# A projection on TensorE: the v channels of the first stage with tokens stationary, and gates as extra columns

## The chip, the cores and the metric

The kernel runs on one core of one Trainium2 chip. The metric is the device time of the whole program in microseconds (us). The core has a matrix engine (TensorE, PE in the profile; PEld is its loading of stationary operands), a vector engine (VectorE, DVE), a scalar engine (ScalarE, ACT) and GpSimd (POOL). SyncE (SP) only issues transfers here. Matmuls write their sums to PSUM, which is used as 8 banks of 128 partitions x 512 fp32 values; all other tiles are in SBUF.

## The reference

One layer of an encoder over two sequences, 1024 and 256 tokens of width 2048. The parts that bear on the change:

```python
hn = rmsnorm(x, norm_w)
proj = einsum('btd,dp->btp', hn, w_in)            # 2048 -> 4*1024 + 5*1024 + 16 columns
na_q, na_k, na_v, na_g, ml_qk, ml_v, ml_o, ml_z, ml_gp = split(proj, ...)
att = neighbourhood_attention(na_q, na_k, na_v, na_rpb) * silu(na_g)
q, k = split(silu(centred_depthwise_conv(ml_qk, conv_w, conv_b)), 2)
gates = ml_gp.reshape(B, T, 2, 2, ML_HEADS) + gate_b           # the 16 columns
mem = rmsnorm(bidirectional_mlstm(q, k, ml_v, gates)) * sigmoid(ml_o) * silu(ml_z)
y = rmsnorm(x + einsum('btm,md->btd', concat(att, mem), w_out), final_norm_w)
```

All data are fp32. na_v and ml_v are 1024 channels each, 2048 v channels together.

## The kernel before

**Precision.** Each fp32 operand of a projection is split into a high part of a reduced format (F32R) and the rest. A product is three matmuls into the same sums: high by high, high by low, low by high. Splitting weights costs a cast on ScalarE (L184) and a subtraction on VectorE (L185, both in `split_a`).

**Stages.** The 1280 tokens are two groups: A with 768 and B with 512. The first stage (up to 1096 us) projects group A to all channels; the second (1096 to 2149 us) projects group B, with the attention and the mLSTM among it; then follows the output projection (L1654).

**A pair.** The first stage goes through the channels in pairs of 128-channel blocks. `pair_a(n1)` computes blocks n1 and n1+1 for all 768 tokens, with the names `A<n1>...` in the profile. It uses a Strassen-like scheme over a 2x2x2 cut (two halves of K, two halves of the tokens, two blocks): seven products, in the order 1, 5, 6, 4, 7, 2, 3, instead of eight. Weights are stationary (128x128) and 384 tokens move. A product has 8 K steps of 3 matmuls, so a pair has 168 matmuls, and its result has channels on partitions. For the products 5, 6, 7 and 3 the weight operand is a sum of raw weights, formed by GpSimd (L531). The sums of tokens are formed once and stay in SBUF; `xop(i, kk, part)` gives the one of product i.

Buffers: raw weights "ra" (3 of 512 KB, one per quarter of K), sums "wt" (4), split weights "wsa" (8), results "pc" (5). A pair holds seven banks, three of tag "pr" and four of the five of tag "a". At the end of K its banks are folded into four result quarters: L498 copies product 1, L494 adds the others, and L263 (`scaled`) multiplies by the tokens' norm.

**What follows a pair.** `finish_a` is a generator, run in steps among the next pair's work. For mLSTM q/k pairs (numbers 24, 26, ... 38) it is the convolution: per block one ScalarE activation, four taps on VectorE (L424), tanh (L429), L430, and a split and store (L180, L181, `store_conv`). For v pairs (56, 58, ... 70) it transposes on TensorE (L470): per 128 tokens two 128x128 transposes into a bank, then `store_v` splits and stores rows of tokens to DRAM.

**Gates.** `gates_a`, called behind the second pair (A6), computes the 16 gate columns of the 768 tokens with 64 wide and 12 small matmuls (L591, L599) and adds the bias (L600). It takes one "ra", four "wsa" and one "pc" buffer.

**Order.** Pairs are issued as 4, 6, and then for i = 0 to 7: q/k pair 24+2i, v pair 56+2i, two others. So A56 comes behind A24, A60 behind A28, and so on. Within this order a planner of the framework interleaves each engine's instructions, by a simulated timeline; dependencies become semaphore waits. The first stage's v in the second stage's form is already in the program for group B: `proj_v` (L769) keeps 128 tokens stationary and moves 256 weight columns, 272 for the unit that has the gates with it. Its results need no transpose.

Of the kernel before, what the change touches and what calls it, by code (L numbers as in the profile page):

```python
# [47 lines left out]
def kernel(  # L48
# [23 lines left out]
    def f(ap):  # L72
        return ap.bitcast(F32)

    def bank(tag, name):
        return ps.tile([P, 512], F32, tag=tag, name=name, bufs=3 if tag == "pr" else 5)
# [103 lines left out]
            S.mul(hi, src, scale)  # L180
            return V.scalar_tensor_tensor(lo, src, scale, f(hi), op0=ALU.mult, op1=ALU.subtract)  # L181

    def split_a(hi, lo, src):
        S.copy(hi, src)  # L184
        last_split["ins"] = V.tensor_tensor(lo, src, f(hi), op=ALU.subtract).ins  # L185

    def q_view(ap):
        return ap.rearrange("p (b r c) -> p r b c", b=4, c=16)
# [44 lines left out]
    def store_v(u, t0, o, src, scale=None):  # L233
        if u >= NA_H // 2:
            hi, lo = o[:, 0], o[:, 1]
        else:
            hi, lo = (o.rearrange("p a (j d) -> p (a j) d", j=2).rearrange(
                "p (j z) d -> p z j d", z=2)[:, z] for z in range(2))
            src = src.rearrange("p (j d) -> p j d", j=2)
        split(hi, lo, src, scale)  # L240
        flat = f(o).rearrange("p a d -> p (a d)")
        if u >= NA_H // 2 or t0 >= TP:
            DM.dma_start(vS[u][t0 : t0 + P], flat)
            return
# [44 lines left out]
        return wa.tile([P, GA], F32, tag="pc", name=name, bufs=NPC)  # L289

    def wsa(name):
        return wa.tile([P, 2, 256], F32R, tag="wsa", name=name, bufs=NWS)

    def first_tiles():
        names = ("pr", "pr", "pr", "a", "a", "a", "a", "a")
# [41 lines left out]
        for kk in range(8):  # L337
            wr = wa.tile([P, 1024], F32, tag="ra", name=f"fr{kk}", bufs=NRA)
            wv = wr.rearrange("p (g j f c) -> p g j f c", g=2, j=2, f=2)
            load(kk, 0)  # L340
            for g_ in range(2):
                DM.dma_start(
                    wv[:, g_],
                    w_in[g_, kk // 2].rearrange("p (j f q c) -> p j f q c", j=2, f=2, q=2)[
                        :, :, :, kk % 2, :
                    ],
                )
            load(kk, 1)
            ws = {}

            def wsplit(h):
                for g_ in range(2):
                    t = wsa(f"fw{kk}_{h}{g_}")
                    hi, lo = (t[:, z].rearrange("p (j c) -> p j c", j=2) for z in range(2))
# [79 lines left out]
    def finish_a(n1, Cn):  # L434
        nm = f"A{n1}"
        for j in range(2):
            if n1 >= NCH:
                break
# [24 lines left out]
        if n1 >= NCH:  # L463
            yield
            yield
            yield
            for tt in range(GA // P):
                b = bank("a", f"{nm}v{tt}")
                for j in range(2):
                    PE.transpose(b[:, j * P : (j + 1) * P], Cn[j][:, tt * P : (tt + 1) * P], ident)  # L470
                if tt in (1, 3):
                    vo = wa.tile([P, GA], F32R, tag="pc", name=f"{nm}vo{tt}", bufs=NPC)
                    vo = vo[:, :512].rearrange("p (a d) -> p a d", a=2)
                else:
                    vo = wa.tile([P, 2, 256], F32R, tag="vo", name=f"{nm}vo{tt}", bufs=1)
                store_v((n1 - NCH) // 2, tt * P, vo, b[:, :256])
                yield

    def pair_a(n1, bg=iter(()), hook=None, first=False, pinned=False):
        nm = f"A{n1}"  # L480
# [37 lines left out]
        for r in range(4):  # L518
# [16 lines left out]
            for i in order:  # L535
# [13 lines left out]
                split_a(t[:, 0], t[:, 1], src[i])  # L549
                for q in range(2):  # L550
                    kk = 2 * r + q
                    mm_c(
# [11 lines left out]
            pass  # L564
        return finish_a(n1, Cn)

    def gates_a():
        raw = wa.tile([P, 1024], F32, tag="ra", name="gAw", bufs=NRA)
        DM.dma_start(raw[:, :256], w_g)
        ab = [raw[:, :P], raw[:, P : 2 * P]]  # L570
        ext = [raw[:, 256 : 256 + P], raw[:, 384 : 384 + P]]
        V.tensor_tensor(ext[0], ab[0], ab[1], op=ALU.add)
        V.tensor_scalar(ext[1], ab[0], -1.0, None, op0=ALU.mult)
        st = []
        for i, src in enumerate((*ab, *ext)):
            t = wsa(f"gAt{i}").rearrange("p h c -> p (h c)")[:, : 8 * 32 + 96]
            G.memset(f(t), 0.0)
            tv = t[:, :256].rearrange("p (k h c) -> p k h c", h=2, c=16)
            sv = src.rearrange("p (k c) -> p k c", c=16)
            split_a(tv[:, :, 0, :], tv[:, :, 1, :], sv)  # L580
            st.append(t)
        sel = raw[0:32, 512:528]
        V.tensor_tensor(sel, ident[0:32, 0:16], ident[0:32, 16:32], op=ALU.add)
        gs = pc("gAg")
        for th, prods in enumerate((((0, 1), (1, 2)), ((2, 3), (3, 7)))):
            b = bank("a", f"gAb{th}")[:, :HALF]
            n = 0
            for w_, i in prods:
                for kk in range(8):
                    for hl_ in range(2):  # L590
                        PE.matmul(  # L591
                            b, st[w_][:, kk * 32 : kk * 32 + P], xop(i, kk, hl_),
                            start=n == 0, stop=n == 31,
                        )
                        n += 1
            V.tensor_copy(gs[0:32, th * HALF : (th + 1) * HALF], b[0:32])
        for tt in range(GA // P):
            b = bank("a", f"gAt{tt}")
            PE.matmul(b[:, :16], gs[0:32, tt * P : (tt + 1) * P], sel, start=True, stop=True)  # L599
            V.scalar_tensor_tensor(  # L600
                gt[:, tt, :], b[:, :16], rcs[0][:, tt : tt + 1], gb_sb, op0=ALU.mult, op1=ALU.add
            )

    opening = first_tiles()
    next(opening)
# [19 lines left out]

    bg = opening
    for i, n1 in enumerate(order):
        bg = pair_a(n1, bg, second_pools if i == len(order) - 1 else None, i == 0, i == 1)
# [109 lines left out]
    def proj_v(u, X):  # L738
# [7 lines left out]
            outs = [pb[t // 2][:, (t % 2) * 256 : (t % 2) * 256 + 256] for t in range(nt)]  # L746
        for r in range(4):
            raw = w_piece(w_in[NCH // 2 + u, r], f"v{u}_{r}")
            rawv = raw.rearrange("p (j f q c) -> p f q j c", j=2, f=2, q=2)
# [5 lines left out]
            for f_ in range(2):  # L755
                t = wb.tile([P, 2, 544], F32R, tag="wsp", name=f"wsv_{u}_{r}_{f_}", bufs=4)
                t4 = t[:, :, : 2 * w].rearrange("p h (k c) -> p h k c", k=2)
                h2, l2 = (
                    t4[:, z, :, 0:256].rearrange("p q (j c) -> p q j c", j=2) for z in range(2)
                )  # L760
                split(h2, l2, rawv[:, f_])
# [979 lines left out]
def _layout(inputs):  # L1741
# [8 lines left out]
    for name, n in (("q", 1024), ("k", 1024), ("v", 1024), ("g", 1024), ("qk", 2048),  # L1750
# [5 lines left out]
    w_in = np.ascontiguousarray(  # L1756
        ch.reshape(2, 4, 2, P, nb // 2, 2, P).transpose(4, 1, 3, 5, 0, 2, 6).reshape(nb // 2, 4, P, 1024)
    )
    gorder = [d * 8 + w_ * 4 + h for w_ in range(2) for d in range(2) for h in range(4)]
    w_g = np.ascontiguousarray(  # L1760
        cols["gp"][:, gorder].reshape(KT, P, 16).transpose(1, 0, 2).reshape(P, KT * 16)
# [65 lines left out]
```

## Time and profile before

| what | value |
|---|---|
| median of 3 runs | 2550.02 us (2548.44 to 2554.36) |
| profiled execution | 2548.95 us |
| span in its profile | 2547.2 us |
| TensorE busy, matmuls | 2527.0 us (99%), 15126 |
| VectorE busy | 1978.3 us (78%) |
| ScalarE busy | 1349.3 us (53%) |
| GpSimd busy | 591.4 us (23%) |
| first stage, second stage, output projection | to 1096, to 2149, to the end |

A row of the chain of waits gives start, length, engine, tile and line, and after the x the number of instructions. A row of the timeline has the same with the operation, what it writes and reads, and the shape; in brackets stands the idle time ahead of it and what ended it. A row of a tile gives the shortest, median and longest duration in ns. Since matmuls overlap in the array, one matmul's recorded duration is longer than the time between two starts.

### The profile page before, as it was taken

The page shows a single profiled execution, that of the slowest core. Times are in us where ns is not written, and L with a number is a line of the kernel's source. Part 1 is how long each engine was busy: PE and PEld are TensorE (multiplying, and loading weights), DVE is VectorE, ACT ScalarE, POOL GpSimd, SP SyncE. Part 2 cuts the span into 40 slices and gives each one's busy share as a digit, 9 for nine tenths or more (in the row PEclk, how much of TensorE's full clock was granted, in tenths as well). Part 3 has the DMA queues.
Part 4 walks back from the last instruction along what each step waited for, and adds up shares of the span by engine and source line. Part 5 has one row for each costly group of instructions (what it writes and reads, how often), then busy time and mean ns, then how long its engine had stood idle before and what let it go on. Part 6 is the DMA issues. An engine that isn't in the chain of part 4 may idle for free.

```text
span 2547.2 us, 44753 instructions
## 1 busy us (share of the span) xinstructions
PE 2527.0 (99%) x15126; PEld 2366.8 (93%) x15126; DVE 1978.3 (78%) x4040; ACT 1349.3 (53%) x3051; POOL 591.4 (23%) x894
## 2 busy tenths in 40 slices
PE   8999999999999999999999999999999999999998
PEld 8999999999999999999999899899898888888886
DVE  8768888898969798988875676776875665889695
ACT  8635545444444444475655665666665653344445
POOL 0434545444444444510000011010100103000001
PEclk9999999999999999999999999999999999999999
DMA  6556474636433343476778888888877849646227
GB/s 216 159 160 206 137 233 132 182 120 192 130 115 128 108 129 100 133 246 210 232 248 270 268 267 288 276 260 272 299 223 242 286 129 356 199 149 211 88 87 256
DMA packets 307757, 505.67 MB, mean 199 GB/s; under 512 B 48992, under 2 KB 195080, under 8 KB 307528
## 3 DMA queue, kind: packets, MB, share of 16 engines
q1 hardware_dynamic: 304568, 491.01, 60.2%
q0 software_dynamic: 2960, 11.80, 1.2%
q8 instruction: 120, 1.97, 0.3%
q14 instruction: 109, 0.89, 0.1%
HBM read 374.18 MB, written 128.52 MB: 197 GB/s over the span
## 4 chain that ended last, share of the span: by engine, by line
PE 83%; DMA 2%; DVE 1%; ACT 1%; issue 0%; SPq 0%; ACTq 0%; POOLq 0%; POOL 0%
PE po L1654 15%; PE pc L686 15%; PE pv L769 5%; PE A16b L286 1%; PE A52b L286 1%; PE A44b L286 1%; PE A40b L286 1%; PE A20b L286 1%; PE A48b L286 1%; PE A50b L286 1%; PE A42b L286 1%; PE A18b L286 1%; PE A14b L286 1%; PE A54b L286 1%; PE A70b L286 1%; PE A68b L286 1%
## 5 line engine op out<-in xcount | busy, mean ns | idle before, releaser
L1654 PE MATMUL po<-wo,mo 128*128 128x512 f32 x1620 | 375.6, 393 | 0.0
L1654 PEld LDWEIGHTS po<-wo,mo 128*128 128x128 f32 x1620 | 304.1, 188 | 70.5
L178 DVE TENSOR_TENSOR ws<-wr,ws 128x512 fp32r<-128x512 f32 x144 | 98.5, 693 | 40.0 <-ACT ws L177 39.5
L177 ACT CAST ws<-wr 128x512 fp32r<-128x512 f32 x144 | 87.6, 617 | 67.7 <-PE pc L686 55.5
L177 ACT CAST mo<-mb 128x640 fp32r<-128x640 f32 x72 | 52.0, 726 | 110.6 <-PE po L1654 100.1
L118 POOL TENSOR_SCALAR rs<-rs 128x1 f32<-128x1 f32 x10 | 4.4, 440 | 373.6 <-DVE rs L1628 373.4
L178 DVE TENSOR_TENSOR mo<-mb,mo 128x640 fp32r<-128x640 f32 x72 | 59.0, 825 | 31.3 <-ACT mo L177 31.3
L1597 DVE TENSOR_TENSOR y<-y,po 128x512 f32<-128x512 f32 x90 | 58.0, 684 | 13.2 <-PE po L1654 13.0
L177 ACT CAST mo<-ms 128x640 fp32r<-128x640 f32 x40 | 28.9, 725 | 50.7 <-PE po L1654 32.6
L178 DVE TENSOR_TENSOR wsv<-wr_v,wsv 128x512 fp32r<-128x512 f32 x64 | 44.6, 702 | 14.1 <-ACT wsv L177 13.9
L177 ACT CAST wsv<-wr_v 128x512 fp32r<-128x512 f32 x64 | 38.9, 617 | 24.5 <-PE pv L769 13.0
L424 DVE SCALAR_TENSOR_TENSOR pcv<-pco,cw_sb,pcv 128x516 f32<-128x516 f32 x48 | 36.5, 760 | 8.5 <-ACT pcv L418 8.5
L1611 ACT ACTIVATE jk<-y 128x512 f32<-128x512 f32 x40 | 25.2, 630 | 29.8 <-DVE y L1597 29.5
L178 DVE TENSOR_TENSOR mo<-ms,mo 128x640 fp32r<-128x640 f32 x40 | 32.9, 823 | 9.8 <-ACT mo L177 9.8
L131 ACT ACTIVATE xq<-xq 128x1024 f32<-128x1024 f32 x20 | 21.2, 1060 | 34.3 <-DMA xq<-in_xtok_dram 32.0
L1110 POOL MEMSET mls_0v<- 128x2 f32 x4 | 0.4, 102 | 162.5 <-DVE S_dt.float L178 137.1
L286 PE MATMUL fb<-xg,fw 128*128 128x384 f32 x192 | 34.6, 334 | 0.0
L286 PEld LDWEIGHTS fb<-xg,fw 128*128 128x128 f32 x192 | 33.4, 188 | 0.0
L807 DVE CUSTOM_DVE_ANT_0 nap_0st<-nap_0s,nap_0bt 128x384 f32<-128x384 f32 x32 | 17.7, 553 | 19.8 <-PE nap_0s L802 7.8
L1560 DVE TENSOR_TENSOR ms<-mb,mb 128x640 f32<-128x640 f32 x40 | 32.9, 823 | 0.0
L263 DVE TENSOR_TENSOR pco<-pc,rstdb 128x512 f32<-128x512 f32 x28 | 19.1, 687 | 16.7 <-PE pc L686 15.8
L810 ACT ACTIVATE nap_0st<-nap_0st,nap_0sm 128x384 f32<-128x384 f32 x32 | 19.8, 617 | 21.9 <-DVE nap_0sm L807 21.9
(2770 smaller groups left out, 8507.5 us busy)
## 6 DMA issues: line engine op xcount, KB each, us to landing
wr<-in_w_in_dram SPq DMA_DIRECT2D x72, 512.0 KB, 4.9
wr_v<-in_w_in_dram SPq DMA_DIRECT2D x32, 512.0 KB, 5.0
wb<-in_w_o_dram SPq DMA_DIRECT2D x48, 256.0 KB, 3.4
xq<-in_xtok_dram SPq DMA_DIRECT2D x20, 512.0 KB, 4.1
mb<-mx POOLq DMA_DIRECT2D x32, 320.0 KB, 7.9
y<-in_xtok_dram SPq DMA_DIRECT2D x35, 256.0 KB, 5.3
wr_wp<-in_w_o_dram SPq DMA_DIRECT2D x16, 512.0 KB, 6.5
vS<-vo SPq DMA_DIRECT2D x24, 256.0 KB, 5.2
```

The lines of the kernel that those rows point to most:

```text
L131: S.activation(raw, raw, AF.Square, accum_out=ssq[g][:, t, q : q + 1])
L177: S.copy(hi, src)
L178: return V.tensor_tensor(lo, src, f(hi), op=ALU.subtract)
L286: PE.matmul(o, w(a_), x(b_), start=first and m == 0, stop=last and m == 2)
L424: V.scalar_tensor_tensor(dst[:, a:n], src[:, a + j - pad : n + j - pad], cw_sb[:, ct, j : j + 1], dst[:, a:n], op0=ALU.mult, op1=ALU.add,)
L686: PE.matmul(pb[j], t[j][:, wi, c : c + P], xs[xi], start=first and m == 0, stop=last and m == 2,)
L769: PE.matmul(outs[tt], xs[:, tt * P : (tt + 1) * P], t[:, wi, q * w : (q + 1) * w], start=first and m == 0 and (gates or tt % 2 == 0), stop ...
L810: S.activation(st, st, AF.Exp, bias=sm[:, 0:1], scale=-1.0, accum_out=sm[:, 2:3])
L1560: V.tensor_tensor(t, x, y_, op=op)
L1597: V.tensor_tensor(Y[p, q, tt], Y[p, q, tt], bk, op=op)
L1611: S.activation(jk, Y[p, q, tt], AF.Square, accum_out=ss[t][:, c : c + 1])
L1654: PE.matmul(bk[tt], m[xi][:, tt * P : (tt + 1) * P], w[wi], start=first and kk == 0 and j == 0, stop=last and j == 2, skip_group_check=True,)
```

## The change

The eight v pairs of the first stage become four units of 512 channels, `unit_v(u, ...)` with u = 0, 2, 4, 6 and names `V<u>...`. A unit takes the place of the pair that had stood there for even i; those of odd i are left out. The same seven products are made with the roles exchanged: 128 tokens (of a half of 384: three tiles) are stationary and 256 weight columns move, so the result has tokens on partitions. A product has 3 tiles x 8 K steps x 3 = 72 matmuls, a unit 504. A tile's 256 columns fill half a bank, and `place` lays a product's third tile beside another product's.

- The products of a unit are made in two passes over K, (1, 5, 6, 7, 3) and then (2, 4), since the banks don't hold all seven. The weights are loaded as 512 KB per K step in two transfers of 1-KB runs (`whole`), and the second half of K again for the last pass.
- V0 also carries the 16 gate columns. They are in the products 1, 2, 3 and 7, whose tiles are then 272 wide and take a bank each. V0 therefore has three passes, (1, 7, 5), (6, 3) and (2, 4), and loads and sums weights anew in the second (`V0p`). For each such product and K step the 16 columns are split apart from the weights (one more ScalarE and one more VectorE instruction). `gate` adds them up with the bias on VectorE.
- `gates_a`, the transposes, and the scaling of v by L263 go. `finish_v` scales by the tokens' norm in the store's split. The gate weights have a buffer of their own.
- The v weights lie in another order in DRAM, and `proj_v` of the second stage reads them without a rearrangement.

```diff
-    order += [QK0 + 2 * i, NCH + 2 * i, *rest[2 * i : 2 * i + 2]]
+    order += [QK0 + 2 * i, *((NCH + 2 * i,) if i % 2 == 0 else ()), *rest[2 * i : 2 * i + 2]]
...
+        if n1 >= NCH:
+            bg = unit_v((n1 - NCH) // 2, bg, gw if n1 == NCH else None)
+        else:
+            bg = pair_a(...)
         if i == 1:
-            gates_a()
+            gw = gate_weights()
...
+    def finish_v(u, z, C):
+        for tt in range(3):
+            t = 3 * z + tt
...
+            store_v(u, t * P, vo, C[:, tt * 256 : (tt + 1) * 256], rcs[0][:, t : t + 1])
+            yield
...
+        def product(i, kk, src, b):
+            t = wsa(f"{nm}s{kk}{i}")
+            split_a(t[:, 0, :256], t[:, 1, :256], src)
+            w = 256
+            if i in G_OF:
+                w = 272
+                split_a(t[:, 0, 256:], t[:, 1, 256:], gw[:, G_OF[i], kk], -1.0 if i == 7 else None)
+            for tt, (o, own, closes) in enumerate(b[i][0]):
+                for m, (xi, wi) in enumerate(((0, 0), (0, 1), (1, 0))):
+                    PE.matmul(
+                        o, xop(i, kk, xi)[:, tt * P : (tt + 1) * P], t[:, wi, :w],
+                        start=kk == 0 and own and m == 0, stop=kk == 7 and closes and m == 2,
+                    )
...
+        for kk in range(8):
+            A, src = whole(kk, "r"), {}
+            for i in passes[0][0]:
+                src[i] = source(i, kk, A, src)
+                product(i, kk, src[i], b)
+                if kk < 7:
+                    if i in (5, 7):
+                        next(bg, None)
+                    continue
+                if i == 1:
+                    for _ in bg:
+                        pass
+                    new(0)
+                    gate(1, b)
+                    for c, o in b[1][1][1:] if gw is None else b[1][1]:
+                        S.copy(C[0][:, c], o)
...
+        if gw is not None:
+            V.tensor_tensor(gw[:, 0], gw[:, 0], gw[:, 1], op=ALU.add)
+            b = {6: place(6, "pr", bank("a", f"{nm}h1")), 3: place(3, ("pr", "pr", "a"))}
+            for kk in range(8):
+                A, src = whole(kk, "p"), {}
+                for i in (5, 6, 3):
+                    src[i] = source(i, kk, A, src)
+                    if i in b:
+                        product(i, kk, src[i], b)
...
+            b = {2: place(2, ("a",) * 3), 4: place(4, "pr", bank("a", f"{nm}h3"))}
```

How the instructions stand is shown at three places; a row is line, operation, written<-read tiles and shape. First, TensorE between A6 and A24. Before, the end of the gate block (`gAb`, `gAt`) stands ahead of A24:

```order
L591 MATMUL gAb_1768<-xg_6_269,gAt_1728 128x384 x2
L591 MATMUL gAb_1768<-xg_7_273,gAt_1728 128x384 x2
L599 MATMUL gAt_1802<-gAw,gAg 128x16
L599 MATMUL gAt_1805<-gAw,gAg 128x16
L599 MATMUL gAt_1808<-gAw,gAg 128x16
L286 MATMUL A24b_1820<-xb_242,A24s_1829 128x384 x3
L286 MATMUL A24b_1820<-xb_246,A24s_1829 128x384 x3
```

Now, on the same engine and at the same place:

```order
L285 MATMUL A6b_1364<-xg_7_271,A6s_1688 128x384 x3
L285 MATMUL A6b_1365<-xg_6_267,A6s_1701 128x384 x3
L285 MATMUL A6b_1365<-xg_7_271,A6s_1701 128x384 x3
L285 MATMUL A24b_1714<-xb_242,A24s_1723 128x384 x3
L285 MATMUL A24b_1714<-xb_246,A24s_1723 128x384 x3
```

A24 follows A6 directly. Second, TensorE at the turn from V0's first pass to its second, now (`V0b` and `V0h` are banks, `V0s` split weights, `xb` and `xg` stationary tokens; bank 2497 is product 6 of the second pass, 2498 to 2500 product 3):

```order
L498 MATMUL V0b_2_2068<-V0s_2454,xg_7_273 128x272 x3
L498 MATMUL V0b_2070<-V0s_2477,xg_7_272 128x256 x6
L498 MATMUL V0h_2069<-V0s_2477,xg_7_272 128x256 x3
L498 MATMUL V0b_2497<-V0s_2508,xg_0_244 128x256 x6
L498 MATMUL V0b_2497<-V0s_2543,xg_1_248 128x256 x6
L498 MATMUL V0b_2497<-V0s_2578,xg_2_252 128x256 x6
L498 MATMUL V0b_0_2498<-V0s_2522,xg_0_243 128x272 x3
L498 MATMUL V0b_1_2499<-V0s_2522,xg_0_243 128x272 x3
```

Before, the same engine at the end of A56, in whose place V0 stands, goes on to the pair A8:

```order
L286 MATMUL A56b_2174<-xg_7_271,A56s_2479 128x384 x3
L286 MATMUL A56b_2175<-xg_6_267,A56s_2492 128x384 x3
L286 MATMUL A56b_2175<-xg_7_271,A56s_2492 128x384 x3
L286 MATMUL A8b_2510<-xb_242,A8s_2519 128x384 x3
L286 MATMUL A8b_2510<-xb_246,A8s_2519 128x384 x3
L286 MATMUL A8b_2511<-xg_0_244,A8s_2531 128x384 x3
L286 MATMUL A8b_2511<-xg_1_248,A8s_2531 128x384 x3
```

What moved: behind the first 216 matmuls, not behind the whole of the v work, TensorE now begins new sums in a bank that was just written. Third, VectorE at that turn, now (`A24cv` is the convolution of A24, `gt` the gates, `V0c` the results of V0):

```order
L423 SCALAR_TENSOR_TENSOR A24cv_2227<-A24c_1973,cw_sb,A24cv_2227 128x766
L178 TENSOR_TENSOR V0s_2522<-gw,V0s_2522 128x16
L178 TENSOR_TENSOR V0s_2543<-V0t_2541,V0s_2543 128x256
L178 TENSOR_TENSOR V0s_2557<-V0t_2555,V0s_2557 128x256
L178 TENSOR_TENSOR V0s_2557<-gw,V0s_2557 128x16
L536 SCALAR_TENSOR_TENSOR gt<-V0b_0_2063,rstdc_229,gb_sb 128x16
L429 SCALAR_TENSOR_TENSOR A24cv_2227<-A24c_1973,A24cv_2227 128x766
L178 TENSOR_TENSOR V0s_2578<-V0t_2576,V0s_2578 128x256
L536 SCALAR_TENSOR_TENSOR gt<-V0b_1_2064,rstdc_229,gb_sb 128x16
```

Before, on the same engine, beside A56:

```order
L424 SCALAR_TENSOR_TENSOR A24cv_2326<-A24c_2079,cw_sb,A24cv_2326 128x766
L185 TENSOR_TENSOR A56s_2492<-A56t_2490,A56s_2492 128x256
L185 TENSOR_TENSOR A8s_2519<-A8r_2517,A8s_2519 128x256
L430 SCALAR_TENSOR_TENSOR A24cv_2326<-A24c_2079,A24cv_2326 128x766
L185 TENSOR_TENSOR A8s_2531<-A8t_2528,A8s_2531 128x256
L185 TENSOR_TENSOR A8s_2543<-A8t_2540,A8s_2543 128x256
L494 TENSOR_TENSOR A56c_2416<-A56c_2416,A56b_2171 128x384
```

The read of V0's first bank (`gt<-V0b_0_2063`) stands behind the taps of A24's convolution. On ScalarE, now, the copies of V0's product 1 to its result stand behind the convolution's last activation:

```order
L428 ACTIVATE A24c_1973<-A24cv_2227 128x766
L177 CAST V0s_2578<-V0t_2576 128x256
L177 CAST V0s_2592<-V0t_2590 128x256
L177 CAST V0s_2592<-gw 128x16
L180 ACTIVATE A24ch_2329<-A24cv_2227 128x766
L573 COPY V0c_2445<-V0b_0_2063 128x256
L573 COPY V0c_2445<-V0b_1_2064 128x256
```

More of the change, by code (lines that the diff above doesn't have):

```diff
@@ L181, in split, with split_a @@
             return V.scalar_tensor_tensor(lo, src, scale, f(hi), op0=ALU.mult, op1=ALU.subtract)
-    def split_a(hi, lo, src):
-        S.copy(hi, src)
-        last_split["ins"] = V.tensor_tensor(lo, src, f(hi), op=ALU.subtract).ins
+    def split_a(hi, lo, src, scale=None):
+        last_split["ins"] = split(hi, lo, src, scale).ins
     def q_view(ap):
@@ L291, in wsa @@
     def wsa(name):
-        return wa.tile([P, 2, 256], F32R, tag="wsa", name=name, bufs=NWS)
+        return wa.tile([P, 2, 272], F32R, tag="wsa", name=name, bufs=NWS)
     def first_tiles():
@@ L353, in wsplit @@
                     t = wsa(f"fw{kk}_{h}{g_}")
-                    hi, lo = (t[:, z].rearrange("p (j c) -> p j c", j=2) for z in range(2))
+                    hi, lo = (t[:, z, :256].rearrange("p (j c) -> p j c", j=2) for z in range(2))
                     split_a(hi, lo, wv[:, g_, :, h, :])
@@ L462, in finish_a @@
             yield
-        if n1 >= NCH:
-            yield
[L465 to L477, printed above, removed]
+    def finish_v(u, z, C):
+        for tt in range(3):
+            t = 3 * z + tt
+            if True:
+                vo = wa.tile([P, GA], F32R, tag="pc", name=f"V{u}o{t}", bufs=NPC)
+                vo = vo[:, :512].rearrange("p (a d) -> p a d", a=2)
+            else:
+                vo = wa.tile([P, 2, 256], F32R, tag="vo", name=f"V{u}o{t}", bufs=1)
+            store_v(u, t * P, vo, C[:, tt * 256 : (tt + 1) * 256], rcs[0][:, t : t + 1])
+            yield
@@ L565, in pair_a, with gate_weights @@
         return finish_a(n1, Cn)
[L567 to L602, printed above, removed]
+    def gate_weights():
+        gw = wa.tile([P, 2, 8, 16], F32, tag="gw", name="gw", bufs=1)
+        DM.dma_start(gw, w_g.rearrange("p (f k c) -> p f k c", f=2, c=16))
+        return gw
     opening = first_tiles()
@@ L748, in proj_v @@
             raw = w_piece(w_in[NCH // 2 + u, r], f"v{u}_{r}")
-            rawv = raw.rearrange("p (j f q c) -> p f q j c", j=2, f=2, q=2)
+            rawv = raw.rearrange("p (f q c) -> p f q c", f=2, q=2)
             if gates:
@@ L757, in proj_v @@
                 t4 = t[:, :, : 2 * w].rearrange("p h (k c) -> p h k c", k=2)
[L758 to L761, printed above, removed]
+                split(t4[:, 0, :, 0:256], t4[:, 1, :, 0:256], rawv[:, f_])
                 if gates:
@@ L1758, in _layout @@
     )
+    vw = w_in[NCH // 2 :].reshape(NU, 4, P, 2, 2, 2, P).transpose(0, 1, 2, 4, 5, 3, 6)
+    w_in[NCH // 2 :] = vw.reshape(NU, 4, P, 1024)
     gorder = [d * 8 + w_ * 4 + h for w_ in range(2) for d in range(2) for h in range(4)]
```

125 lines of the change are left out of this document (121 added, 4 removed).

## The prediction

> **What bounds the kernel now.** I read the page first: the busy shares, the granted clock and the make-up of the chain that ended last.
>
> ```profile
> span 2547.2 us, 44753 instructions
> PE 2527.0 (99%) x15126; PEld 2366.8 (93%) x15126; DVE 1978.3 (78%) x4040; ACT 1349.3 (53%) x3051; POOL 591.4 (23%) x894
> PEclk9999999999999999999999999999999999999999
> PE 83%; DMA 2%; DVE 1%; ACT 1%; issue 0%; SPq 0%; ACTq 0%; POOLq 0%; POOL 0%
> ```
>
> TensorE is the bound, at an undisturbed clock. That is an average, so next comes the stage that the change touches, by windows (times of busy engines, then clock, DMA share, GB/s):
>
> ```profile
> core 0: us, PE busy (x) PEld busy (x) DVE busy (x) ACT busy (x) POOL busy (x), PEclk, DMA share, GB/s
> 138.10:150.10 12.00, 12.00 (x72) 11.75 (x70) 8.63 (x20) 3.69 (x9) 2.95 (x4) 1.00 0.55 157
> 176.90:214.10 37.20, 37.20 (x217) 37.20 (x216) 36.68 (x61) 18.47 (x43) 17.99 (x18) 1.00 0.39 114
> 269.00:1068.00 799.00, 798.80 (x4631) 796.95 (x4630) 674.08 (x1209) 381.49 (x913) 380.15 (x435) 1.00 0.45 141
> ```
>
> From 269 to 1068 us TensorE rests for 0.2 us in all. So each matmul added or taken away there counts in full, and another engine counts only where it falls behind far enough to stop TensorE. The second row is the stretch in which pair A24's convolution runs beside the first v pair, A56: VectorE has 36.68 of 37.20 us full there. It is the one place of the stage with no reserve on VectorE, and the changed unit V0 stands on it.
>
> **The matmuls.** Since matmuls overlap, a price is time between starts, read from unbroken pieces of the chain (start, length, what, matmuls):
>
> ```profile
> 388.02 29.13 PE A28b L286 x168
> 417.15 29.13 PE A60b L286 x168
> ...
> 1096.03 8.13 PE pv L769 x66
> ...
> 1200.27 2.72 PE S32bx L1408 x24
> ...
> 1368.37 10.60 PE pv L769 x90
> ```
>
> A pair, v or not, takes 29.13 us for 168 matmuls of 384 columns, 173.4 ns each. The second stage already has the form that the units take (tokens stationary, weights moving): 10.60/90 = 117.8 ns for 256 columns and 8.13/66 = 123.2 ns for 272.
>
> - Removed: eight v pairs, 8 x 29.13 = 233.0 us.
> - Added: 4 units x 504 = 2016 matmuls. Four products of V0 are 272 wide (4 x 72 = 288), the other 1728 are 256 wide: 288 x 0.1232 + 1728 x 0.1178 = 35.5 + 203.5 = 239.0 us.
>
> So the products alone lose 6.0 us, because the fixed part of a narrow matmul is paid more often. The ends: at the 113.3 ns of the S32bx row (256 wide, but weights stationary) they cost 231.3, a gain of 1.7; were all as dear as the 272-wide ones, 248.4, a loss of 15.4. I take the pv rows, the same form with the same kind of operands.
>
> **Transposes.** The v pairs leave channels on partitions and are transposed in six groups of two. The groups of one pair, first and last, stand in the chain:
>
> ```profile
> 455.72 0.22 PE A60v L470 x2
> ...
> 478.66 0.22 PE A60v L470 x2
> ```
>
> 8 x 6 x 0.22 = 10.6 us go. The scaling by the tokens' norm (L263) goes into the store's split, where it is a factor per partition; that takes work off VectorE, which is worth nothing by itself.
>
> **Gates.** The old gate block lies on TensorE between A6 and A24:
>
> ```profile
> 138.14 2.95 PE L591 MATMUL gAb<-xb,gAt 128*128 128x384 f32 x16
> ...
> 149.38 0.84 PE L599 MATMUL gAt<-gAw,gAg 32*128 32x16 f32 x6
> 150.15 1.32 PE L286 MATMUL A24b<-xb,A24s 128*128 128x384 f32 x6
> ...
> 153.70 0.84 PE L599 MATMUL gAt<-gAw,gAg 32*128 32x16 f32 x6
> 154.46 1.86 PE L286 MATMUL A24b<-xg,A24s 128*128 128x384 f32 x9
> ```
>
> 149.38 - 138.14 = 11.2 us of wide matmuls and (150.15 - 149.38) + (154.46 - 153.70) = 1.5 of small ones: 12.7 us go. The 16 columns that replace them are in the 239.0. While this block ran, VectorE was 8.63 of 12.00 us busy, so A24's weights had 11 us in which to arrive and be split. Without it A24 begins right behind A6; I cost that at nothing, since the gate weights no longer take one of the three raw-weight buffers and A24's own loads move up. Were that cover gone, one load's way would show:
>
> ```profile
> fr<-in_w_in_dram SPq DMA_DIRECT2D x16, 256.0 KB, 5.6
> ```
>
> up to 5.6 us. TensorE's part is then 239.0 - 233.0 - 10.6 - 12.7 = **-17.3 us**.
>
> **V0's first handover.** V0's first pass (products 1, 7, 5) holds all eight banks, and the second pass needs a bank that is empty only when the gate row and the copy to C0 have read it. In front of them, on VectorE, stands the convolution of A24. TensorE is through the first pass in 144 x 0.1232 + 72 x 0.1178 = 26.2 us, where A56 gave VectorE 29.13.
>
> ```profile
> 176.86 0.54 DVE L494 TENSOR_TENSOR A24c<-A24c,A24b 128x384 f32<-128x384 f32 x1
> ...
> 186.11 0.41 DVE L185 TENSOR_TENSOR A56s<-A56r,A56s 128x256 fp32r<-128x256 f32 x1
> 186.44 0.96 DVE L185 TENSOR_TENSOR A56s<-A56t,A56s 128x256 fp32r<-128x256 f32 x1
> ...
> 207.21 1.12 DVE L430 SCALAR_TENSOR_TENSOR A24cv<-A24c,A24cv 128x766 f32<-128x766 f32 x1 [0.29 <-ACT A24c L429]
> ...
> 213.18 0.95 DVE L181 SCALAR_TENSOR_TENSOR A24c<-A24cv,A24ch 128x766 f32<-128x766 f32 x1
> ```
>
> ```profile
> L286 PE MATMUL A56b<-xb,A56s x24: 331/335/342, 180.6 to 203.3; 128*128 128x384 f32 x24
> L185 DVE TENSOR_TENSOR A56s<-A56t,A56s x16: 410/414/959, 175.4 to 206.2; 128x256 fp32r<-128x256 f32 x16
> L494 DVE TENSOR_TENSOR A56c<-A56c,A56b x7: 539/543/545, 208.9 to 215.3; 128x384 f32<-128x384 f32 x7
> L531 POOL TENSOR_TENSOR A56t<-A56r x8: 737/800/1440, 168.3 to 195.7; 128x256 f32<-128x256 f32 x8
> L180 ACT ACTIVATE A24ch<-A24cv x2: 846/848/851, 196.5 to 209.0; 128x766 fp32r<-128x766 f32 x2
> L600 DVE SCALAR_TENSOR_TENSOR gt<-gAt,rstdc,gb_sb x6: 211/222/234, 150.0 to 154.9; 128x16 f32<-128x16 f32 x6
> L498 ACT COPY A56c<-A56b x1: 462/462/462, 207.1 to 207.1; 128x384 f32<-128x384 f32 x1
> ```
>
> VectorE takes up A24's folding 3.6 us before TensorE turns to A56 (176.86 against 180.5; call that turn T) and ends the last convolution operation at 214.1, 37.2 us later. Behind V0 the same stretch has five fewer splits of weights (5 x about 0.55, between the 0.41 and 0.96 of the rows) and no six A56c adds (6 x 0.54), but 17 splits of 16 columns and 6 gate rows (23 x 0.22) and one sum of gate weights (about 0.2): 37.2 - 2.7 - 3.3 + 5.1 + 0.2 = 36.5. Behind the first gate row some 3.9 us of it remain, so that row runs at T + 36.5 - 3.6 - 3.9 = T + 29.0; then come L430 (0.95 undisturbed), ScalarE's hi part (0.85) and the C0 copy (0.36, the 0.46 of a 384-wide one scaled), 2.3 with the row itself: T + 31.3. TensorE, done at T + 26.2, waits 5.1.
>
> The rows also say what would lengthen this. A split between two buffers of SBUF takes 0.41 or, while GpSimd adds weights, 0.96; the adds out of PSUM stay at 0.54. By then 26 sums have been made on GpSimd instead of the window's 18; if each stretches one VectorE operation by 0.41, the row is late by 3.3 more and the wait is 8.4. [...]
>
> Between 5.1 and 8.4 I take **7**, nearer the upper end since most sums fall beside splits in the rows. The bounds are 0 (the planner brings the copy ahead of the convolution) and 12 (both stretched further).
>
> **The other handovers.** V0's second pass makes three sums per step on GpSimd, 2.2 to 2.4 us at 0.74 to 0.80, where TensorE needs 18 matmuls, nine of each width, 2.17. That is 0.3 to 1.9 us over eight steps; I cost it at nothing, because the wait ahead of it lets up to four steps' splits be made in advance, and at the 1.9 if that cover is gone. V2, V4 and V6 give the convolution 360 x 0.1178 = 42.4 us of cover in their first pass, so none waits for it. At their second pass the bank of product 5 is wanted 27 matmuls behind product 7 (3.2 us); VectorE empties it with the last of three 512-wide adds and a 256-wide one, and two splits stand between.
>
> ```profile
> L1597 DVE TENSOR_TENSOR y<-y,po 128x512 f32<-128x512 f32 x90 | 58.0, 684 | 13.2 <-PE po L1654 13.0
> ```
>
> 3 x 0.68 + 0.41 (scaled from the 0.54 of 384 columns) + 2 x 0.41 to 0.96 = 3.3 to 4.4, so 0.1 to 1.2 us. Since the splits can move behind the adds I put 0.3 on each, 1 in all, between 0 and 3.6.
>
> The v stores have 256-wide operations once per token tile, with the reserve on VectorE (674 of 799). Weights are read 512 KB per 5.3 us in a normal unit, 99 GB/s, and up to 240 GB/s for some 17 us in V0's second pass, against 141 in the window above. The second stage is not changed in order, only its layout of v weights, which gives longer runs.
>
> **The sum.** -17.3 + 7 + 1 = -9.3. The profiled execution took 2548.95 us, 1.07 below the median of 2550.02, so it comes to 2539.6 there, and **2540.5** with the median as base.
>
> **Rivals.**
> - *No wait at V0.* The wait hangs on 5 us of VectorE's order. If the copy to C0 is run earlier, the sum is -16 (2534); with 256 columns at the S32bx price, -25 (2525). Against it: VectorE at 36.68 of 37.20.
> - *V0's second pass bound by its sums or loads.* The wait at 8.4, then sums at 1.0 us (the row's maximum is 1.44) instead of 0.74: 8 x (3.0 - 2.17) = 6.6, and 3 for the other units: -17.3 + 18 = +0.7, 2551. Three raw buffers of 512 KB in parts of 256 KB with 5.6 us to landing speak for it, the four steps made ahead against it.
> - *Slower: the banks.* All eight banks are in use in each pass, where a pair uses seven of eight and leaves by folds one at a time. If each of the two handovers of V2, V4 and V6 costs 2.8 us rather than the 0.15 put on them, that is 16 us: 2556 and above; past 2.6 us each (14.4/6 more) it is slower by over 0.2%. For it: folds and splits share VectorE's queue, and a split may stand behind 4 us of adds. Against it: eight split buffers, so TensorE has ready weights for a few steps in hand.
>
> **Chances.** About 0.2% (5 us) is what a measurement of this kernel can tell from no change. Forecast, 2535 to 2545: 0.48. No wait, 2524 to 2535: 0.19. V0's second pass bound, 2545 to 2555: 0.20. Banks, 2555 to 2572: 0.13. Faster 0.67, same 0.20, slower 0.13. Left out of the range are the ends of the first and last case, down to 2526 and up from 2556.
>
> **What would show it.** In the changed profile: starts of V2b 118 ns apart and of V0b's wide ones 123; no gAb and no A56v; a rest of TensorE of 5 to 8 us ahead of V0b's second pass, released by the C0 copy; A24 right behind A6b; V2's, V4's and V6's passes without a rest over 0.5 us; a second stage of the same length. The forecast is wrong if 256 columns cost over 121 ns, if rests recur in the normal units, or if A24's start waits for weights.

## The result, and the profile after

The changed kernel takes 2554.01 us (median of 22 runs) against 2550.75 us before (22 runs): a ratio of 1.0013, with a 95% interval of 1.0008 to 1.0019. The forecast was 2540.5, faster; the kernel is slower by 0.13%, inside the forecast's range and on the wrong side. The profiled execution shown below took 2554.88 us, 5.9 more than the one of before, where the medians differ by 3.3; so some 2.7 us of what follows is scatter between executions.

The page of the changed kernel: span, busy shares, clock, and the chain's shares.

```profile
span 2553.2 us, 45865 instructions
PE 2524.8 (99%) x15626; PEld 2363.0 (93%) x15626; DVE 1982.5 (78%) x4045; ACT 1351.6 (53%) x3080; POOL 616.4 (24%) x898
PEclk9999999999999999999999999999999999999999
PE 78%; DVE 4%; DMA 1%; issue 1%; ACT 1%; SPq 0%; POOL 0%; ACTq 0%; POOLq 0%; DVEq 0%
```

TensorE is busy 2.2 us less than before, where the forecast took 17.3 off it, and VectorE's share of the chain has gone from 1 to 4%. Two different losses hide in this: TensorE stops for VectorE, and its matmuls themselves became dearer.

**The rest that was forecast.** Timeline of TensorE at the turn from V0's first pass to its second, and of VectorE and ScalarE ahead of it (start, length, engine; in brackets idle time and releaser):

```profile
195.83 0.52 PE L498 MATMUL V0h<-V0s,xg 128*128 128x256 f32 x3
202.69 5.45 PE L498 MATMUL V0b<-V0s,xg 128*128 128x256 f32 x30 [6.35 <-DVE gt L536]
```

```profile
199.96 0.22 DVE L536 SCALAR_TENSOR_TENSOR gt<-V0b,rstdc,gb_sb 128x16 f32<-128x16 f32 x1
...
200.11 1.40 DVE L429 SCALAR_TENSOR_TENSOR A24cv<-A24c,A24cv 128x766 f32<-128x766 f32 x1
...
201.54 0.84 ACT L180 ACTIVATE A24ch<-A24cv 128x766 fp32r<-128x766 f32 x1 [0.99 <-DVE A24cv L429]
202.29 0.91 ACT L573 COPY V0c<-V0b 128x256 f32<-128x256 f32 x3
```

The chain is the one of the working: gate row, L429 (the kernel before has it as L430), ScalarE's hi part, copy to C0, and the rest is 6.35 us where 7 was taken. What was not in the working comes behind it. Windows of the rest, of the stretch behind it, and of the next:

```profile
core 0: us, PE busy (x) PEld busy (x) DVE busy (x) ACT busy (x) POOL busy (x), PEclk, DMA share, GB/s
196.20:202.60 6.40, 0.14 (x2) 0.00 (x0) 6.40 (x12) 3.22 (x9) 5.30 (x7) 0.75 0.44 140
202.60:206.00 3.40, 3.31 (x15) 3.31 (x16) 3.40 (x9) 1.31 (x6) 3.24 (x4) 0.50 0.77 247
206.00:209.00 3.00, 3.00 (x26) 3.00 (x25) 3.00 (x10) 0.41 (x2) 2.03 (x4) 0.97 0.90 278
```

After the rest the granted clock is 0.50 for 3.4 us, and 15 matmuls of 256 columns go through in them, 214 ns from start to start instead of 118: another 1.5 us. The window that begins 3.3 us after the restart has 0.97. The prediction did not weigh that. In the second stage of the same profile 3.4 us at 0.50 follow a rest of only 1.81 us. A row of the timeline, and a window with the columns above:

```profile
1655.62 0.76 PE L928 MATMUL nap_0s<-nap3qk 128*128 128x384 f32 x3 [1.81 <-DMA nap3qk<-kS]
1656.85:1660.26 3.41, 3.41 (x19) 3.41 (x17) 3.20 (x10) 1.95 (x6) 1.78 (x6) 0.50 1.07 397
```

**The pairs, which the change seems not to touch.** The chain of the changed kernel (start, length, what, matmuls), three pairs that wait for nothing:

```profile
478.71 29.33 PE A16b L285 x168
508.04 29.41 PE A18b L285 x168
537.45 29.35 PE A30b L285 x168
```

Before, a pair took 29.13 us. Now nearly every one takes 29.33 to 29.41, with no wait in it. That is 174.6 to 175.1 ns a matmul instead of 173.4, at a granted clock of 1.00.

**The other units.** Window of V4, from its first matmul to that of the next pair; then TensorE and VectorE at the end of V2's first pass:

```profile
654.80:716.20 61.40, 60.95 (x506) 60.09 (x506) 55.82 (x93) 29.52 (x70) 30.81 (x31) 1.00 0.47 154
```

```profile
447.53 0.28 PE L498 MATMUL V2b<-V2s,xg 128*128 128x256 f32 x1
448.05 0.86 PE L498 MATMUL V2b<-V2s,xg 128*128 128x256 f32 x5 [0.24 <-DVE V2s L178]
...
450.68 0.88 PE L498 MATMUL V2b<-V2s,xb 128*128 128x256 f32 x5 [0.21 <-DVE V2s L178]
```

```profile
447.04 1.29 DVE L178 TENSOR_TENSOR V2s<-V2t,V2s 128x256 fp32r<-128x256 f32 x2
...
448.26 1.49 DVE L181 SCALAR_TENSOR_TENSOR A28c<-A28cv,A28ch 128x766 f32<-128x766 f32 x1
...
449.66 0.96 DVE L178 TENSOR_TENSOR V2s<-V2r,V2s 128x256 fp32r<-128x256 f32 x1
...
450.54 2.51 DVE L178 TENSOR_TENSOR V2s<-V2t,V2s 128x256 fp32r<-128x256 f32 x4
```

Each unit takes 61.3 to 61.4 us instead of 504 x 117.8 = 59.4. TensorE stops four or five times late in the first pass, for splits of weights that stand behind A28's last convolution operations on VectorE. The first matmul behind each stop is dearer as well (220 to 226 ns from start to start); by the starts in the trace the ten long gaps of V2 are 1.7 us above 118 ns each.

The account by the two profiles, all against the forecast of -9.3:

| where | forecast | measured | difference |
|---|---|---|---|
| to A24's first matmul (150.15 before, 140.18 now) | -12.0 | -10.0 | +2.0 |
| pairs from A24 on (945.7 before with 8 v pairs, 706.4 now) | -244.3 | -239.3 | +5.0 |
| V0 (60.9 and the wait of 7) | +67.9 | +69.8 | +1.9 |
| V2, V4, V6 (178.1 and 1) | +179.1 | +184.1 | +5.0 |
| second stage, to the output projection's first matmul | 0 | +1.3 | +1.3 |
| sum | -9.3 | +5.9 | +15.2 |

### The profile page after: what moved, and what is told of

It reads as the page before. It is cut to its first block, busy times and chain, and to the rows that moved or that the text cites. A ratio compares the mean times of both kernels' runs of the same rounds, so it can differ in the third digit from the quotient of the medians.

```text
span 2553.2 us, 45865 instructions
## 1 busy us (share of the span) xinstructions
PE 2524.8 (99%) x15626; PEld 2363.0 (93%) x15626; DVE 1982.5 (78%) x4045; ACT 1351.6 (53%) x3080; POOL 616.4 (24%) x898
## 4 chain that ended last, share of the span: by engine, by line
PE 78%; DVE 4%; DMA 1%; issue 1%; ACT 1%; SPq 0%; POOL 0%; ACTq 0%; POOLq 0%; DVEq 0%
PE pc L815 16%; PE po L1780 15%; PE pv L895 6%; PE A52b L285 1%; PE A44b L285 1%; PE A50b L285 1%; PE A42b L285 1%; PE A20b L285 1%; PE A18b L285 1%; PE A22b L285 1%; PE A38b L285 1%; PE A34b L285 1%; PE A30b L285 1%; PE A54b L285 1%; PE A46b L285 1%; PE A48b L285 1%
## 5 line engine op out<-in xcount | busy, mean ns | idle before, releaser
L498 PE MATMUL V0b<-V0s,xg 128*128 128x272 f32 (+1 forms) x360 | 50.3, 291 | 6.4 <-DVE gt L536 6.4
L498 PEld LDWEIGHTS V0b<-V0s,xg 128*128 128x128 f32 x360 | 47.6, 195 | 6.6 <-ACT V0c L573 6.6
L498 PE MATMUL V6b<-V6s,xg 128*128 128x256 f32 x288 | 42.4, 282 | 0.2 <-DVE V6s L178 0.2
L498 PE MATMUL V4b<-V4s,xg 128*128 128x256 f32 x288 | 42.4, 282 | 0.2 <-DVE V4s L178 0.2
L498 PE MATMUL V2b<-V2s,xg 128*128 128x256 f32 x288 | 42.4, 282 | 0.2 <-DVE V2s L178 0.2
L498 PEld LDWEIGHTS V4b<-V4s,xg 128*128 128x128 f32 x288 | 37.6, 188 | 0.6 <-DVE V4s L178 0.4
```

The source lines that it names most:

```text
L498: PE.matmul(o, xop(i, kk, xi)[:, tt * P : (tt + 1) * P], t[:, wi, :w], start=kk == 0 and own and m == 0, stop=kk == 7 and closes and m == 2,)
```

## The experiments

**Where the dearer pairs come from.** The tile of split weights became 272 wide, for V0's gate columns, and every pair uses the same tiles. First that, in the kernel before, with seven such tiles in place of eight to make room:

```diff
-NRA, NWS, NWT, NPC, NPO = 3, 8, 4, 5, 6
+NRA, NWS, NWT, NPC, NPO = 3, 7, 4, 5, 6
...
-        return wa.tile([P, 2, 256], F32R, tag="wsa", name=name, bufs=NWS)
+        return wa.tile([P, 2, 272], F32R, tag="wsa", name=name, bufs=NWS)
...
-                split_a(t[:, 0], t[:, 1], src[i])
+                split_a(t[:, 0, :256], t[:, 1, :256], src[i])
```

> The kernel before with one thing of the change alone: the tile of split weights has rows of 272 instead of 256 columns, of which the pairs use 256 (to have room, seven such tiles instead of eight). Theory A, the distance of 1088 instead of 1024 bytes between the parts of a split weight is what makes each 384-wide matmul dearer: the pairs of the first stage go from 29.13 to about 29.4 us, and the program gets 6 to 10 us longer (34 pairs x 0.2 to 0.3). Rival B, the dearer pairs after the change come from the granted clock or from neighbours in time: pairs stay at 29.13 and the time within 2 us of before.

2565.08 us, ratio 1.0056 (1.0041 to 1.0071). Two pairs in the chain of its profile, one of them a v pair:

```profile
394.40 29.39 PE A28b L286 x168
423.79 29.39 PE A60b L286 x168
```

Pairs went from 29.13 to 29.39 us with not a matmul changed, 34 x 0.26 = 8.8 us of the 14.5. The missing eighth tile is in the time too (A8 and A12 took 2.0 and 1.2 us more), and the second stage of its profile was 4.4 us longer. The opposite test takes the wide tiles from the pairs of the changed kernel:

```diff
-        return wa.tile([P, 2, 272], F32R, tag="wsa", name=name, bufs=NWS)
+        return wa.tile([P, 2, 256], F32R, tag="wsa", name=name, bufs=5)
+
+    def wsg(name):
+        return wa.tile([P, 2, 272], F32R, tag="wsg", name=name, bufs=3)
...
-            t = wsa(f"{nm}s{kk}{i}")
+            t = (wsg if i in G_OF else wsa)(f"{nm}s{kk}{i}")
```

> The changed kernel, but only V0's 272-wide products use wide tiles (three of them, a buffer of their own), all other weights tiles of 256 columns (five). Theory A: pairs return to 29.13 us, 24 x 0.25 = 6 us less in the first stage, and the 256-wide matmuls of V2, V4, V6 fall below 118 ns, toward 113 to 116 (up to 1512 x 4 ns = 6 us more); V0's rest may grow by some us with fewer tiles in advance. In all 4 to 10 us less than after the change. Rival B: pairs stay at 29.35 to 29.41 us.

```profile
598.20 29.13 PE A22b L285 x168
```

The pair's price is back to 29.13 us where a pair waits for nothing, so it is not the number of tiles and not the granted clock (0.998 over the run, as in the run above). The time was 2582.44 us, 1.0131 (1.0116 to 1.0146): five tiles are too few for the pairs, and the opening and the pairs beside convolutions wait for splits; by its profile the second stage was 8.3 us longer than after the change as well. The expected gain of 4 to 10 us was wrong by that. That the 256-wide matmuls of the units got cheaper is not shown either: the 288 of V4b that read `xg` kept TensorE busy for 45.1 us, against 42.4 after the change.

Then the form of the address. Parts of 256 columns lie side by side (1024 bytes apart), in tiles that still begin every 2176 bytes:

```diff
-        return wa.tile([P, 2, 272], F32R, tag="wsa", name=name, bufs=NWS)
+        return wa.tile([P, 544], F32R, tag="wsa", name=name, bufs=NWS)
+
+    def halves(t, w=256):
+        return t[:, : 2 * w].rearrange("p (h c) -> p h c", h=2)
```

> The changed kernel with the two parts of a 256-wide split weight side by side (1024 bytes apart) in the same tiles of 2176 bytes, so that a tile's start is a multiple of 128 bytes and not of 512. Theory A in its narrow form, that what matters is a start on a multiple of 128 bytes: pairs return to 29.13 us, 6 us less than after the change. In its wide form, that multiples of 512 bytes are needed: pairs stay at 29.3 to 29.4 us for three tiles of four, the time as after the change within 2 us. Rival B: no change either.

```profile
566.06 29.30 PE A20b L285 x168
595.36 29.29 PE A22b L285 x168
```

2551.55 us, 1.0007 (0.9998 to 1.0017). Pairs that wait for nothing take 29.29 to 29.30, so starts on multiples of 128 bytes were not enough here, and the change is no longer distinguishable from no change. V0 took 1.2 us longer than after the change (71.1 against 69.8). These 174.4 ns are a mean over a pair. By the starts in the traces, A30's matmuls before the change stand 173 or 174 ns apart in 164 of 167 cases, and A22's after it anywhere from 168 to 184; what sets the single gap stays open. Two further runs, on the kernel with the units moved and the halves side by side (below), made the tiles 2304 bytes (9 x 256) and 2560 bytes (5 x 512), with room made elsewhere:

```diff
-NRA, NWS, NWT, NPC, NPO = 3, 8, 4, 5, 6
+NRA, NWS, NWT, NPC, NPO = 3, 8, 3, 5, 6
...
-        return wa.tile([P, 544], F32R, tag="wsa", name=name, bufs=NWS)
+        return wa.tile([P, 576], F32R, tag="wsa", name=name, bufs=NWS)
```

> As with the units moved and the halves side by side, but tiles of 2304 instead of 2176 bytes (9 x 256), so that every tile starts on a multiple of 256 bytes; to have room, three tiles for sums of weights instead of four. If starts on multiples of 256 bytes are enough, pairs take 29.13 us instead of 29.29, 24 x 0.16 = 4 us less, about 2540 unless the missing tile for sums costs some of it; if multiples of 512 are needed, half of the tiles profit, 29.2 us and about 2542; if it isn't the start, 29.3 and 2544.

> The same with tiles of 2560 bytes (5 x 512), of which only seven fit. If it is the start and the distance on multiples of 512 bytes, pairs take 29.13 us wherever TensorE doesn't wait for splits; the missing eighth tile costs at the opening and behind the convolutions (with seven wide tiles in the kernel before, A8 and A12 took 1.6 to 2 us more than with eight). About 2541 to 2546. If pairs stay at 29.3, neither start nor distance is the cause.

Chain of the one with 2304 bytes:

```profile
536.30 29.13 PE A30b L285 x168
565.43 29.13 PE A20b L285 x168
594.56 29.13 PE A22b L285 x168
```

With 2304 bytes 18 of 24 pairs take 29.13 us, and with 2560 bytes 17. So in these runs a pair's matmul cost 173.4 ns with tiles every 2304 or 2560 bytes, 174.4 with tiles every 2176 and 1024 between the parts, and 174.6 to 175.1 with tiles every 2176 and 1088 between the parts. Counted from the first tile, the weights then start on multiples of 256, 512, 128 and 64 bytes; where the first tile lies is not on record. The times did not follow: 2548.16 us (0.9986; 0.9977 to 0.9996) and 2561.39 us (1.0038; 1.0024 to 1.0052). With one tile less for sums V0 took 2.5 us longer than with 2176-byte tiles and A18 2 us, and with seven split tiles A14 3 us. The second stages of the two profiles were 3.4 and 7.6 us longer than with the units moved and 2176-byte tiles. The clock may be part of both times: its mean over the profiled execution was 0.998 with 2304 bytes and 0.997 with 2560, against 0.999 with the units moved, the halves side by side and 2176-byte tiles. Beyond that no cause was found.

**What stops the units.** V0 one place later, behind A8, so that A24's convolution runs beside A8:

```diff
-        order += [QK0 + 2 * i, *((NCH + 2 * i,) if i % 2 == 0 else ()), *rest[2 * i : 2 * i + 2]]
+        order += [QK0 + 2 * i, *((NCH + 2 * i,) if i in (2, 4, 6) else ()), rest[2 * i]]
+        order += [*((NCH,) if i == 0 else ()), rest[2 * i + 1]]
```

> The changed kernel with V0 one place later, behind pair A8 instead of A24, so that A24's convolution runs beside A8 and V0 has A8's short store of q/k beside it. Theory: the rest of TensorE ahead of V0's second pass (6.4 us) falls below 1 us, and with it the stretch behind it in which matmuls took 214 ns at a granted clock of 0.50 (1.5 us): 7 to 8 us less than after the change. Rival: the second pass waits for its own sums on GpSimd and for its loads, and the rest stays at 3 us or more, or turns up in pieces within the second pass.

TensorE at the same turn:

```profile
225.61 0.52 PE L498 MATMUL V0h<-V0s,xg 128*128 128x256 f32 x3
227.56 1.47 PE L498 MATMUL V0b<-V0s,xg 128*128 128x256 f32 x10 [1.43 <-ACT V0c L573]
```

The rest is 1.43 us instead of 6.35, the first ten matmuls behind it go through in 1.30 us from start to start (130 ns each, where it was 214), V0 takes 64.2 us instead of 69.8, and the program 2549.00 us: 0.9996 (0.9986 to 1.0005), some 5 us less than after the change. So the convolution made the rest; 1.4 us remain, more than expected, and A26 got 1.3 us longer, which gives part of it back. The rival (sums or loads of the second pass) is not seen. Now all four units one place later:

```diff
-        order += [QK0 + 2 * i, *((NCH + 2 * i,) if i % 2 == 0 else ()), *rest[2 * i : 2 * i + 2]]
+        order += [QK0 + 2 * i, rest[2 * i], *((NCH + 2 * i,) if i % 2 == 0 else ()), rest[2 * i + 1]]
```

> The changed kernel with all four units one place later, behind a pair that isn't followed by a convolution. Theory: the 1.3 to 1.7 us by which V2, V4 and V6 stop late in their first pass come from splits that stand behind the convolution's last operations on VectorE; so each takes 59.6 to 60 us instead of 61.4, and V0 64.2 as when it alone was moved: 9 to 10 us less than after the change, about 2544.5, faster than before by 0.2 to 0.3%. Rival: they come from the folding of seven banks at the end of the pass, which is unchanged: V2, V4, V6 stay at 61.4 and the time at 2549.

V4 and V6 take 60.4 and 60.5 us (from 61.4 and 61.3), V2 61.3. So the convolution accounts for about 1 us in V4 and V6; in V2, which has rests at its start instead, the move brought nothing. The profiled execution took 2546.29, the median was 2549.98 us (2543.76 to 2552.27): 0.9992 (0.9983 to 1.0001), a gain of 4 instead of the expected 9 to 10.

Then this together with the halves side by side:

> Units one place later and the two parts of a 256-wide split weight side by side, together. If the two effects add: 59.8 us per unit and pairs at 29.29, 2.5 us less than with the units moved alone, about 2542.

2544.09 us, 0.9979 (0.9969 to 0.9988): faster than before by 0.2%, 10 us less than after the change, and the best version here. The window of its V4:

```profile
677.05:736.89 59.84, 59.58 (x505) 59.37 (x505) 45.53 (x83) 26.06 (x64) 27.17 (x33) 1.00 0.48 152
```

59.84 us against the 59.4 of the forecast's price, with VectorE busy 45.5 of it instead of 55.8 of 61.4. The units' moving weights lie in the same tiles. In the trace after the change, with 1088 bytes between the parts, the undisturbed 256-wide matmuls of V2, V4 and V6 stand 118.5 to 118.6 ns apart in the mean. Here, with 1024, 207 of V4's stand 116.9 apart (682.44 to 706.64 us), where the same ones after the change, without their stops, stand 118.3 apart.

**The two halves of the change apart.** Units at the change's places, the gates in their old block, V0 in two passes like the others, all tiles 256 wide:

```diff
-            bg = unit_v((n1 - NCH) // 2, bg, gw if n1 == NCH else None)
+            bg = unit_v((n1 - NCH) // 2, bg)
...
-            gw = gate_weights()
+            gates_a()
```

> The v part of the change alone: units as in the changed kernel and at its places, V0 in two passes like the others, gates in the old block behind A6, all split weights in tiles of 256 columns. Theory: pairs at 29.13 us (6 us less than after the change), V0 61.4 instead of 69.8 (8.4 less), the gate block back (12.7 more): 1 to 2 us less than after the change, about 2552; so the gates as columns and their third pass bring nothing here. Rival, that the wide tiles are not what the gates cost: 2556 or more.

> The same with the units one place later. If the convolution is what stops the units: each 1.6 us shorter, 6.4 us less than with the gates apart alone, about 2546; if not, 2552.

With the gates apart: 2554.36 us, 1.0015 (1.0006 to 1.0024). Chain and V4's window:

```profile
569.07 29.13 PE A20b L285 x168
598.20 29.13 PE A22b L285 x168
```

```profile
656.30:717.50 61.20, 60.70 (x505) 59.81 (x505) 55.64 (x93) 29.43 (x70) 30.59 (x31) 1.00 0.47 152
```

Pairs are at 29.13 again and V0 at 61.2 us, as expected, and the gate block takes its 12.0 us. The first stage ended 0.8 us earlier than after the change, where 1 to 2 were expected; the program's time can't be told from the changed kernel's. So the v part alone already loses: from A24 on the first stage takes 948.9 us in place of 945.7. Its four units take 244.8 us; the eight v pairs took 233.0, and their transposes with the waits beside them made other pairs 12.2 us longer than 29.13. That alone would be even, but other pairs are longer than 29.13 here too, by 3.7 us in all (A10 and A14 by 0.8 and 1.2, in part waits for splits). And the gates as columns gain 12.0 in the gate block and 1.4 in A24, among whose matmuls the block's last small ones stood, and lose 8.6 in V0 (69.8 - 61.2) and 24 x 0.25 = 6.0 in the pairs, 14.6 in all. With the units moved it is 2552.78 us, 1.0010 (1.0001 to 1.0019): V4 and V6 at 60.3 and 60.4, V0 and V2 at 61.6 and 61.5, so 1.0 us less in all four instead of 6.4.

**A last version** with eight tiles that all start on multiples of 256 bytes, in two rings:

```diff
+    turn = cycle("nwnnwnnw")
+
+    def wsa(name, kind=None):
+        if (kind or next(turn)) == "w":
+            return wa.tile([P, 576], F32R, tag="wsw", name=name, bufs=3)
+        return wa.tile([P, 512], F32R, tag="wsa", name=name, bufs=5)
```

> Units moved, and eight tiles of split weights in two rings, five of 2048 bytes and three of 2304; pairs take them in turn, V0's 272-wide products only the three. All tiles start on multiples of 256 bytes and there are eight again, with four tiles for sums. Theory: pairs at 29.13 us, so 24 x 0.16 = 4 us less than with the units moved and halves side by side (2544), about 2540 to 2541; V0 may take 1 to 3 us more with three tiles for its wide products. If the pairs' price is all there is, it's faster than before by 0.3 to 0.4%.

2547.75 us, 0.9987 (0.9978 to 0.9996). Pairs are at 29.13 us (15 of 24) and all 24 together 2.6 us shorter than with 2176-byte tiles; but V0, with three tiles for its wide products, takes 69.1 us instead of 64.7; and the second stage of its profile is 2.7 us longer. The mean granted clock of its profiled execution was 0.997, against 0.999. It does not beat 2544.09.

## Why the prediction was wrong

- **The matmuls.** The prices held where nothing disturbs: a unit undisturbed but for one stop took 59.84 us, 118.7 ns a matmul, against 117.8 taken, and the 272-wide ones stood 125 ns apart at the median, against 123.2. So the products on TensorE are as they were worked out, up to the stops and the shared tile below.
- **Transposes and gates** went as forecast, the gates with -12.0 ahead of A24; the transposes were worth 12.2 rather than 10.6, by the pairs' lengths before (A20 and A22, behind a v pair, took 30.39 and 29.35 us). Of the gates' gain 2.0 came back before A24. The same opening took 1.8 us less with the units moved, where nothing ahead of A24 is changed (A24 at 138.38 instead of 140.18), so most of this is taken for scatter of the opening; that is not shown.
- **V0's first handover**: right in place, mechanism and size (6.35 against 7; 5.1 to 8.4 bounded). The first gate row came at T + 30.4 instead of T + 29.0: 16-column splits of the gate weights took 0.43 us at the median rather than 0.22, and the sum of gate weights 0.82 rather than 0.2. Missing was the half clock behind it, 1.5 us.
- **The step that failed first: "The other handovers", 1 us.** "V2, V4 and V6 give the convolution 42.4 us of cover in their first pass, so none waits for it" took VectorE's total for its order. The planner spreads the convolution over the whole pass, and its last operations of 1.0 to 1.5 us stand ahead of splits that TensorE needs at once. The units lost 6.0 us (184.1 - 178.1) where 1 was put. Moving them showed about 1 us of it each for V4 and V6; which part of V2's loss is the convolution's stays open.
- **The step that was missing altogether: the width of the shared tile.** The working followed the 272-wide tile only into V0. All 24 pairs read their weights from it, and each became 0.2 to 0.3 us longer, 6.0 us in all, a term that the sum had at nothing. (The 5.0 in the table is this and 1.4 of waits in A10 and A14, less what the transposes and A24's small gate matmuls gave beyond the forecast.) Alone in the kernel before it does the same, and it goes away (29.13 us) with tiles every 2304 bytes.
- **The second stage** was to keep its length; it was 1.3 us longer. In the runs of this study it lay between 1053 and 1055 us with eight split tiles of the old or the changed size in the first stage, before and after alike, so this is not told from scatter. The profile does show the rest of 1.81 us and the half clock behind it there; before, the same load was waited for 0.54 us, at full clock. The 1056 to 1063 us of the kernels with fewer tiles or with two rings were not explained.
- **The rivals.** The slower one had TensorE lose 2.8 us at each of two handovers of three units. The loss per unit was 2.0 in all, by splits and not by banks. V0's second pass was not bound by its sums or loads: behind the rest V0 shows no stop of note. The time landed where the second rival put it, for another reason.

The two wrong steps, 6.0 and 4 to 5 us, with the 1.5 of the clock, are some 12 us of the 13.5 between 2540.5 and 2554.0. (The sum's -9.3 from the median of 2550.02 is 2540.7; the text has 2540.5.)

## What to carry to other kernels

When a change resizes a shared buffer, follow it to every reader of that buffer: here 64 more bytes of stride in each part cost 6.0 us in the pairs, where the wider matmuls that needed them cost V0 some 288 x 7 ns = 2.0 us. "Enough cover in the pass" must be checked against the order in which the slow engine does its work, because the bound engine stops for the one late item, not for the total. And a rest of TensorE cost more than its length here: 1.5 us more behind the 6.35 us, and behind 1.81 us there were 3.4 us at a clock of 0.50.

## What was not expected of the hardware

- The mean time between the matmuls of a pair (384 columns) went with where its stationary weights lie in SBUF: 173.4 ns with tiles every 2304 bytes, 174.4 with tiles every 2176 and 1024 between the parts, 174.6 to 175.1 with tiles every 2176 and 1088 between the parts. Which unit causes it was not tested, and the single gaps are not explained by it.
- After the rest of 6.35 us TensorE ran at a granted clock of 0.50 for about 3.4 us, and 3.4 us at 0.50 also followed the rest of 1.81 us in the changed kernel's second stage. Behind the 1.43 us with V0 moved ten matmuls took 130 ns each, and behind the 0.54 us in the second stage before the clock stayed at 1.00. What decides it is not shown.
- In V2, V4 and V6 of the changed kernel, five matmuls of each first pass start late, 162 to 521 ns behind the one before; the next one starts 220 to 227 ns later instead of 118.
